# Decode hand-outs of a hybrid decoder step: 28 places for the first sequence's key pages, and a later start of the second set

## The chip, the cores and the metric

The kernel runs on one core of a Trainium2 chip. The time is device microseconds (us) of one execution. The engines of a core work from queues of their own and meet through semaphores: TensorE (PE, matrix products and transposes; PEld is its weight load), VectorE (DVE), ScalarE (ACT), GpSimd (POOL), and SyncE (SP), which here issues most DMA transfers. The profiler also shows the clock that TensorE was granted (PEclk, 1.00 is full).

## The reference

A step of a two-layer decoder: 1024 prompt tokens with 16 meta tokens in front, and 8 running sequences with one new token each. Layer 0 mixes by gated linear attention (GLA), layer 1 by differential attention; each is followed by a squared-ReLU MLP, and each sum by a LayerNorm:

```
x = post_norm(x, mixer(x), ln_mix_g, ln_mix_b)      # layer_norm(ALPHA*x + f)
x = post_norm(x, relu(x @ w1)**2 @ w2, ln_mlp_g, ln_mlp_b)
...
k_past = cache_k[page_table].reshape(B, past, DIFF_HEADS, 2, DIFF_DH)
v_past = cache_v[page_table].reshape(B, past, DIFF_HEADS, DIFF_DV)
o = diff_core(q, [k_past | k], [v_past | v], ...)   # both softmaxes, then their difference
```

The part that the change touches is the last of these for the 8 running sequences ("decode"): each has 32 pages of 128 past keys and 32 pages of values, 1024 float32 numbers to a row, in a cache that a page table addresses. That is 256 key pages and 256 value pages of 512 KB each. The scores are taken against one query row, softmax goes over all 4096 past positions and the own one, and the values are summed with the weights.

## The kernel before

**Order of the program.** First GLA and the few-token work of the running sequences (through both layers up to the projections of layer 1, so that decode's queries exist early), then for the prompt: `w_out` of GLA (L887), a LayerNorm (`normalize`), the first MLP (`mlp`, L978), a LayerNorm, layer 1's projection (the loop over 12 units of 256 columns that ends with `next(paged, None)`), the prompt's attention (`prep` and `tile_`, from L1105 on), and layer 1's own output product and MLP. Products are made in float32 out of three passes (`mm3`, L185 to L188): each operand is split into a high and a low part, the rest is taken by a subtraction (`split`, L183 on DVE: `XH`/`XL` for activations, `HH`/`HL` for the MLP's hidden values; for weights L174 on POOL, `wlo`, after ACT's L173, `whi`).

**Decode runs beside this work.** `decode()` (L848) is a generator. For each sequence b it makes `k_start` (the query row `qb` in all partitions), the softmax of the sequence before it (`soft`, L792), and then 32 turns. A turn takes one key page of b and one value page of b-1. A key page (`k_page`, L782) is a DMA of 512 KB through SP, whose address SP reads from the page table first (L756, then L758), one product with the query (L789; on POOL for every fourth page, otherwise on DVE), and one reduction to 16 scores (L790, on DVE). A value page is one DMA and four matmuls of 256 columns (`v_pages`, L830), issued for two pages at a time and tied behind the key reduction of the same turn. Key and value pages share one pool (`pgp`) of 8 tiles. After the last sequence `v_end` (L836) moves the sums out; the pool is given back (`de.close()`) before the prompt's attention begins, whose buffers lie in the same room.

**What sets the order.** A scheduler lays the instructions of each engine out by priority and by its own reckoning of when each could start. Nearly all of decode stands at a priority behind everything else ("background"), so that it fills what others leave. Two things pull it back:

- *Hand-outs.* At a `yield` the generator stops until the main program calls `next` on it. `w_out` calls it after each of its first 5 tiles, the first down run of the MLP after every second of its 16 tiles (8 calls), and then `next(x for x in side if x)` lets decode run without a stop until the next `yield` that gives a nonzero b. Between that and the next place, decode is "free": its pages are issued in one go, at background priority. The projection hands out one turn per tile from its first tile on, and what is left after the last `yield` is free again.
- *Order behind a step.* `tc.issue_after(ins)` keeps an instruction behind `ins` in the schedule. A handed-out page's product stands behind the newest entry of `steps_v` (DVE's steps of the main program) or `steps_g` (POOL's).

The hand-outs are: pages 0 to 11 of sequence 0 at 13 places (5 and 8); pages 12 to 199 free, in the first MLP; pages 200 to 215 (sequence 6, turns 8 to 23) at 16 places in the projection; pages 216 to 255 and the value pages of the last sequence free after that. `HOLD = (6, 8)` says where the second set begins.

**Other lines that matter below.** In the MLP's first round (`g == 0`) DVE also multiplies the residual `Y` by `ln_mix_g` (`alpha_row`, L970), four times two instructions, each pair after a DMA of a row of weights into `ht`, which has one buffer. The LayerNorm takes statistics of `Y` on DVE (L923, L927, L931), a power on POOL (L932), the shift on DVE (L936), and applies both on ACT (L938). PE then transposes the result (L949), which ACT or DVE (L953) scale and DVE splits (L183). L1014 adds a product to `Y` in the MLP's down runs. `prep` (L1105) transposes keys and queries of a head on PE (L1134 for the 16 meta rows, L1139 keys, L1144 queries) with a `split` behind each; `tile_` multiplies them (L1174 to L1176) into scores, which DVE masks (L1182) with the tile `cmask`, set at L1102 in room that decode had.

Of the kernel before, what the change touches and what calls it, by code (L numbers as in the profile page):

```python
# [30 lines left out]
NPG = 32  # L31
# [2 lines left out]
NEG = -1e30  # L34
LAM_INIT = 0.8 - 0.6 * math.exp(-0.3)
PGB = 8
HOLD = (6, 8)
HTB = 1
LEVELS = (64, 32, 16, 8, 4, 2, 1)
ROPE_INV = 500000.0 ** (-np.arange(0, 16, 2, dtype=np.float64) / 16)  # L40
# [70 lines left out]
def hybrid_step(ctx, tc, A, dbg=None, upto=9):  # L111
# [69 lines left out]
    def split(hi, lo, src, eng=V):  # L181
        S.copy(hi, src)
        return eng.tensor_tensor(lo, src, hi.bitcast(F32), op=ALU.subtract)  # L183
# [55 lines left out]
    ps = smt()  # L239
# [15 lines left out]
    for c in range(2):  # L255
        for k in range(NB):
            ps = axt()
            for i in range(4):
                TE.transpose(ps[:, i * P : (i + 1) * P], Yt[:, 4 * c + i, k * P : (k + 1) * P], ident)
            cs = slice(512 * c, 512 * c + 512)  # L260
# [13 lines left out]
    ps = smt()  # L274
# [46 lines left out]
    for c in range(2):  # L321
        ps = mmt()
# [55 lines left out]
    ps = smt()  # L378
# [4 lines left out]
    ps = smt()  # L383
# [8 lines left out]
    ps = smt()  # L392
# [4 lines left out]
    for h in range(GH):  # L397
        m = log_gate(ps[:, h * TS : (h + 1) * TS], TS, h)
# [23 lines left out]
    ps = smt()  # L422
# [5 lines left out]
    for hh in range(2):  # L428
        ps = smt()
# [8 lines left out]
    ps = smt()  # L438
# [4 lines left out]
    for s in (8, 4, 2, 1):  # L443
        u = t2()[:, :128]
        level(sb.rearrange("p h t -> p (h t)"), sqk[:, :128], sqk[:, 128:], u, s, V)
        ps = smt()
# [46 lines left out]
    ps = smt()  # L493
# [61 lines left out]
    for half in range(2):  # L555
        ps = smt()
# [54 lines left out]
    for h in range(GH):  # L611
# [7 lines left out]
        for c in range(2):  # L619
            q, k_, v = qk[c, 0], qk[c, 1], Yh[:, h, 4 * c : 4 * c + 4, :]  # L620
            cs = slice(512 * c, 512 * c + 512)
            m = log_gate(pgs[c], 512, h)
            b = g2.tile([P, 512], F32, name="gb")
# [159 lines left out]
    def k_page(b, n, sc, qb):  # L783
        with background():
            pg = page("cache_k", b, n)
            eng, after = (G, steps_g) if n % 4 == 3 else (V, steps_v)

            with tc.issue_after(after[-1]) if (b == 0 and n < 24 and after) or (b == HOLD[0] and HOLD[1] <= n) else nullcontext():
                eng.tensor_tensor(pg, pg, qb, op=ALU.mult)  # L789
            return V.tensor_reduce(sc[:, n, :], pg.rearrange("p (h d) -> p h d", d=64), op=ALU.add, axis=AX.X).ins  # L790

# [56 lines left out]
    def decode():  # L848
        ks = None
        for b in range(NS + 1):  # L850
            prev = ks
            if b < NS:
                ks = k_start(b)
            if b > 0:
                w = soft(prev[0])
                acc = smt()
            held, k = [], None
            for n in range(NPG):
                if b == 0 or (b == HOLD[0] and HOLD[1] <= n < HOLD[1] + 16):
                    yield b  # L860
                if b < NS:
                    k = k_page(b, n, *ks)
                if b > 0:

                    if len(held) == 2:
                        v_pages(held, w, acc, k)
                        held = []
                    held.append((n, v_load(b - 1, n)))
            if b > 0:
                held.append((NPG, v_load(b - 1, NPG)))  # L870
                v_pages(held, w, acc, None)
                v_end(b - 1, acc)
# [9 lines left out]
    def w_out(w, scaled, side=None):  # L882

        units = {}
        n = 0
        for u, c in ((0, 0), (1, 0), (0, 1), (1, 1), (2, 0), (3, 0), (2, 1), (3, 1)):
            if u not in units:  # L887
                units[u] = kunit(w, u * 256)
            hv, lv = (x.rearrange("p (k n) -> p k n", n=256) for x in units[u])
            for i2 in range(2):  # L890
                ps = mmt()
                t0 = 4 * c + 2 * i2
                for i in range(2):
                    a = slice((t0 + i) * P, (t0 + i + 1) * P)
                    for k in range(NB):
                        mm3(ps[:, i * 256 : (i + 1) * 256], XH[:, k, a], XL[:, k, a], hv[:, k, :], lv[:, k, :], k == 0, k == NB - 1)
                yv = Yt[:, t0 : t0 + 2, u * 256 : (u + 1) * 256]
                pv = ps.rearrange("p (i n) -> p i n", n=256)
                if scaled:
                    V.tensor_tensor(yv, yv, pv, op=ALU.add)  # L900
                else:
                    steps_v.append(V.scalar_tensor_tensor(yv, yv, ALPHA, pv, ALU.mult, ALU.add).ins)
                if side and (n == 4 if scaled else n < 5):
                    next(side)
                n += 1
                if u % 2:
                    for t in (t0, t0 + 1):
                        yield t, u // 2
# [66 lines left out]
    def mlp(side):  # L975

        w1, w2 = A["mlp_w1"][0], A["mlp_w2"][0]
        for g in range(8):  # L978
            us = [None, None]
            order = [(u, c) for c in range(2) for u in range(2)] if g == 0 else [(u, c) for u in range(2) for c in range(2)]  # L980
            for u, c in order:
                if us[u] is None:
                    us[u] = kunit(w1, g * 512 + u * 256)
                hv, lv = (x.rearrange("p (k n) -> p k n", n=256) for x in us[u])
                cs = slice(512 * c, 512 * c + 512)
                for m in range(2):
                    ps = mmt()
                    ms = slice(m * P, (m + 1) * P)
                    for k in range(NB):
                        mm3(ps, hv[:, k, ms], lv[:, k, ms], XH[:, k, cs], XL[:, k, cs], k == 0, k == NB - 1)  # L990
                    S.activation(ps, ps, AF.Relu)
                    S.activation(ps, ps, AF.Square)
                    split(HH[:, 2 * u + m, cs], HL[:, 2 * u + m, cs], ps)
            if g == 0:
                with tc.issue_after(steps_v[-1]):
                    list(alpha_row(A["ln_mix_g"][0:1], ALU.mult))
                beta = alpha_row(A["ln_mix_b"][0:1], ALU.add)
            elif g < 5:
                next(beta)
            us = [None, None]  # L1000
            if g < 7:
                order = [(u, t) for u in range(2) for t in range(8)]
            else:
                order = [(u, t) for u in range(2) for t in range(4)] + [(u, t) for t in range(4, 8) for u in range(2)]
            for n, (u, t) in enumerate(order):
                if us[u] is None:
                    us[u] = unit(512, w2[g * 512 : (g + 1) * 512, u * 512 : (u + 1) * 512].rearrange("(k p) n -> p k n", p=P))
                hv, lv = (x.rearrange("p (k n) -> p k n", n=512) for x in us[u])
                ps = mmt()
                ts_ = slice(t * P, (t + 1) * P)  # L1010
                for k in range(4):
                    mm3(ps, HH[:, k, ts_], HL[:, k, ts_], hv[:, k, :], lv[:, k, :], k == 0, k == 3)
                yv = Yt[:, t, u * 512 : (u + 1) * 512]
                steps_v.append(V.tensor_tensor(yv, yv, ps, op=ALU.add).ins)  # L1014
                if g == 0 and n % 2 == 0:
                    next(side, None)
                if g == 7:
                    yield t, u
            if g == 0:
                next(x for x in side if x)  # L1020
# [551 lines left out]
```

## Time and profile before

| | |
|---|---|
| time, 3 runs (us) | median 2921.13 (2912.52 to 2928.78) |
| profiled execution, its span (us) | 2919.7 |
| PE busy | 2779.7 (95%) |
| DVE busy | 1891.2 (65%) |
| ACT busy | 1044.1 (36%) |
| POOL busy | 1133.7 (39%) |
| DMA | 636.46 MB, mean 218 GB/s |
| 256 key pages, 256 value pages | 512.0 KB each, 6.0 us from issue to landing (median) |
| POOL's page products, L789 | 64, 158.6 us, mean 2478 ns |
| DVE's page products, L789 | 192, 256.8 us, mean 1343 ns |
| DVE's page reductions, L790 | 256, 309.7 us, mean 1214 ns |

The busy share of PE is an average over stages: where PE is the bound, nothing that another engine does costs time; the time that decode costs shows as idle time of PE, as a lowered clock after it, and as decode's own matmuls. By the line numbers, `w_out` and its LayerNorm run up to about 640 us, the first MLP from there to about 1457 us, the projection from about 1457 to 1785 us, and the attention begins at 1785 us. Line numbers in the profile before are those of the code above; in the changed kernel, lines from 994 on lie 4 higher (L1014 becomes L1018, L1139 becomes L1143, L1174 becomes L1178).

### The profile page before, as it was taken

How to read it: one execution, taken by the hardware profiler on the slowest of the kernel's cores; microseconds unless marked ns; L12 is line 12 of the kernel's file. 1: busy time of each engine (PE TensorE's matmuls, PEld its weight loads, DVE VectorE, ACT ScalarE, POOL GpSimd, SP SyncE). 2: the span in 40 equal slices, each digit the busy share in tenths (PEclk: the TensorE clock that was granted, in tenths of full speed). 3: DMA queues.
4: the chain of work that ended last, by engine and by line, in shares of the span. 5: the costliest groups of instructions: out<-in, count | busy, mean ns of one | idle time of the engine just before them, and what ended most of it. 6: DMA issues, size and time to landing. Idle time of an engine off the chain costs nothing. (4 is left out here: it accounts for less than half of the span.)

```text
span 2919.7 us, 52085 instructions
## 1 busy us (share of the span) xinstructions
PE 2779.7 (95%) x19653; PEld 2277.6 (78%) x19653; DVE 1891.2 (65%) x2982; ACT 1044.1 (36%) x2075; POOL 1133.7 (39%) x867
## 2 busy tenths in 40 slices
PE   8889999999999999999999998889998999999997
PEld 5666767987777777777898896778888889797885
DVE  2564644457877777777667942788638855838478
ACT  3233453251222122122321112667524535335352
POOL 2230222233333334334233331132335766677664
PEclk9899999999999999999999998999999999999998
DMA  7557651514798988988387999363436778595893
GB/s 257 178 185 251 233 177 37 198 56 141 242 350 297 335 309 298 346 317 321 137 275 252 348 343 314 75 139 86 119 112 205 195 207 232 152 281 129 257 246 87
DMA packets 285366, 636.46 MB, mean 218 GB/s; under 512 B 25510, under 2 KB 141292, under 8 KB 273852
## 3 DMA queue, kind: packets, MB, share of 16 engines
q1 hardware_dynamic: 252716, 520.66, 51.6%
q0 software_dynamic: 32400, 112.50, 15.9%
q8 instruction: 154, 2.52, 0.4%
q14 instruction: 96, 0.79, 0.1%
HBM read 575.55 MB, written 44.06 MB: 212 GB/s over the span
## 5 line engine op out<-in xcount | busy, mean ns | idle before, releaser
L174 POOL TENSOR_TENSOR wlo<-raw,whi 128x512 fp32r<-128x512 f32 x256 | 360.0, 1419 | 744.0 <-ACT whi L173 670.8
L186 PE MATMUL mmt<-whi,XH 128*128 128x256 f32 (+1 forms) x1760 | 527.4, 302 | 2.9 <-ACT Y L310 2.0
L187 PE MATMUL mmt<-wlo,XH 128*128 128x256 f32 (+1 forms) x1760 | 527.8, 301 | 0.7 <-POOL wlo L174 0.7
L186 PE MATMUL mmt<-XH,whi 128*128 128x512 f32 (+1 forms) x1216 | 438.1, 361 | 7.4 <-DVE HL L183 7.2
L188 PE MATMUL mmt<-whi,XL 128*128 128x256 f32 x1536 | 437.2, 286 | 0.1
L188 PE MATMUL mmt<-XH,wlo 128*128 128x512 f32 (+1 forms) x1216 | 434.4, 358 | 0.0
L790 DVE TENSOR_REDUCE sc<-pg 128x16 f32<-128x1024 f32 x256 | 309.7, 1214 | 93.4 <-POOL pg L789 90.1
L173 ACT CAST whi<-raw 128x512 fp32r<-128x512 f32 x256 | 152.9, 619 | 578.4 <-PE mmt L188 191.1
L186 PEld LDWEIGHTS mmt<-whi,XH 128*128 128x128 f32 x1760 | 333.4, 190 | 30.1 <-issue 15.6
L187 PEld LDWEIGHTS mmt<-wlo,XH 128*128 128x128 f32 x1760 | 334.8, 190 | 28.2 <-issue 16.8
L187 PE MATMUL mmt<-XL,whi 128*128 128x512 f32 x768 | 307.3, 400 | 0.0
L188 PEld LDWEIGHTS mmt<-whi,XL 128*128 128x128 f32 x1536 | 292.1, 191 | 9.9 <-issue 8.8
L789 DVE TENSOR_TENSOR pg<-pg,qb 128x1024 f32<-128x1024 f32 x192 | 256.8, 1343 | 62.1 <-DMA pg<-in_cache_k 38.1
L186 PEld LDWEIGHTS mmt<-XH,whi 128*128 128x128 f32 x1216 | 231.7, 191 | 55.1 <-issue 13.7
L789 POOL TENSOR_TENSOR pg<-pg,qb 128x1024 f32<-128x1024 f32 x64 | 158.6, 2478 | 293.5 <-DMA pg<-in_cache_k 236.7
L188 PEld LDWEIGHTS mmt<-XH,wlo 128*128 128x128 f32 x1216 | 231.8, 191 | 35.8 <-issue 3.8
L186 PE MATMUL mmt<-whi,HH 128*128 128x512 f32 x512 | 205.6, 402 | 1.7 <-DVE Y L1014 1.7
L187 PE MATMUL mmt<-wlo,HH 128*128 128x512 f32 x512 | 204.7, 400 | 0.0
L188 PE MATMUL mmt<-whi,HL 128*128 128x512 f32 x512 | 203.9, 398 | 0.0
L187 PEld LDWEIGHTS mmt<-XL,whi 128*128 128x128 f32 x768 | 145.4, 189 | 39.6 <-issue 8.8
L1416 POOL TENSOR_TENSOR wlo<-RW,whi 128x512 fp32r<-128x512 f32 x96 | 156.3, 1749 | 37.1 <-ACT whi L1415 37.0
L1416 POOL TENSOR_TENSOR wlo<-rw,whi 128x512 fp32r<-128x512 f32 x92 | 147.7, 1674 | 41.4 <-ACT whi L1415 41.2
(441 smaller groups left out, 5769.3 us busy)
## 6 DMA issues: line engine op xcount, KB each, us to landing
pg<-in_cache_k SPq DMA_DIRECT2D x256, 512.0 KB, 6.0
pg<-in_cache_v SPq DMA_DIRECT2D x256, 512.0 KB, 6.0
XH<-xc POOLq DMA_DIRECT2D x42, 1032.0 KB, 7.9
raw<-in_mlp_w SPq DMA_DIRECT2D x164, 256.0 KB, 3.5
swt<-in_mlp_w SPq DMA_DIRECT2D x32, 1024.0 KB, 5.6
rw<-in_mlp_w SPq DMA_DIRECT2D x116, 256.0 KB, 3.8
RW<-in_mlp_w POOLq DMA_DIRECT2D x96, 256.0 KB, 6.0
xc<-XH POOLq DMA_DIRECT2D x14, 1032.0 KB, 6.8
```

The source lines that it names most:

```text
L173: S.copy(hi[:, c], raw)
L174: G.tensor_tensor(lo[:, c], raw, hi[:, c].bitcast(F32), op=ALU.subtract)
L186: TE.matmul(ps, ah, bh, start=first, stop=False)
L187: TE.matmul(ps, ah, bl, start=False, stop=False)
L188: TE.matmul(ps, al, bh, start=False, stop=last)
L789: eng.tensor_tensor(pg, pg, qb, op=ALU.mult)
L790: return V.tensor_reduce(sc[:, n, :], pg.rearrange("p (h d) -> p h d", d=64), op=ALU.add, axis=AX.X).ins
L1416: G.tensor_tensor(lo[:, k, :], t, hi[:, k, :].bitcast(F32), op=ALU.subtract)
```

## The change

```diff
-HOLD = (6, 8)
+HOLD = range(232, 248)
...
-            with tc.issue_after(after[-1]) if (b == 0 and n < 24 and after) or (b == HOLD[0] and HOLD[1] <= n) else nullcontext():
+            with tc.issue_after(after[-1]) if (b == 0 and n < 28 and after) or HOLD.start <= NPG * b + n < NPG * (HOLD.start // NPG + 1) else nullcontext():
                 eng.tensor_tensor(pg, pg, qb, op=ALU.mult)
...
-                if b == 0 or (b == HOLD[0] and HOLD[1] <= n < HOLD[1] + 16):
+                if b == 0 or NPG * b + n in HOLD:
                     yield b
...
-                if side and (n == 4 if scaled else n < 5):
+                if side and (n == 4 if scaled else n < 12):
                     next(side)
...
         for g in range(8):
             us = [None, None]
+            normed = steps_v[-1]
...
                     S.activation(ps, ps, AF.Square)
-                    split(HH[:, 2 * u + m, cs], HL[:, 2 * u + m, cs], ps)
+                    i = split(HH[:, 2 * u + m, cs], HL[:, 2 * u + m, cs], ps).ins
+                    if g == 0:
+                        steps_v.append(i)
+                        next(side)
             if g == 0:
-                with tc.issue_after(steps_v[-1]):
+                with tc.issue_after(normed):
                     list(alpha_row(A["ln_mix_g"][0:1], ALU.mult))
```

`w_out` hands out after its first 12 tiles, the MLP's first up run after each of its 8 tiles, its first down run after 8 tiles as it did. So 28 places, after which pages 0 to 26 are issued and the free run goes from page 27 to page 231. The second set, 16 places at the same tiles of the projection, is pages 232 to 247 (sequence 7, turns 8 to 23), and 248 to 255 with the last sequence's values come free after it. The up run's subtractions become steps behind which a page's product may stand, and `normed` keeps the L970 rows behind the step that they stood behind before, the last before the MLP. The amount of work is the same.

What stands in the queues, at three places (buffer numbers in the names are the program's).

PE at the end of the projection, before: the last L186 to L188 rows are the projection's, `smt<-pg,sc` at L830 are value pages (four matmuls each), L1134 to L1144 head 0's and then head 1's transposes.

```order
L188 MATMUL mmt<-whi,XL_86 128x256
L1134 MATMUL axt<-c_ident,whi 128x16
L1139 MATMUL axt<-c_ident,wlo 128x128 x4
L830 MATMUL smt<-pg,sc 16x256 x4
L1144 MATMUL axt<-c_ident,wlo 128x128 x4
L830 MATMUL smt<-pg,sc 16x256 x4
L1139 MATMUL axt<-c_ident,wlo 128x128 x4
L830 MATMUL smt<-pg,sc 16x256 x4
L1144 MATMUL axt<-c_ident,wlo 128x128 x4
L830 MATMUL smt<-pg,sc 16x256 x4
L1174 MATMUL mmt<-XH_83 128x352
```

And in the changed kernel:

```order
L188 MATMUL mmt<-whi,XL_86 128x256
L1138 MATMUL axt<-c_ident,whi 128x16
L1143 MATMUL axt<-c_ident,wlo 128x128 x4
L1148 MATMUL axt<-c_ident,wlo 128x128 x4
L1143 MATMUL axt<-c_ident,wlo 128x128 x4
L1148 MATMUL axt<-c_ident,wlo 128x128 x4
L1178 MATMUL mmt<-XH_83 128x352
```

No value page is left behind the projection; the last ones stand before its last 912 matmuls.

DVE in the MLP's first up run, before (HL at L183 is what PE's down run waits for, L970 the residual's rows):

```order
L183 TENSOR_TENSOR HL<-mmt,HH 128x512
L953 TENSOR_SCALAR axt<-axt,lnp 128x512
L183 TENSOR_TENSOR XL_86<-axt,XH_84 128x512 x2
L970 SCALAR_TENSOR_TENSOR Y<-Y,ht 128x4x256 x6
L183 TENSOR_TENSOR HL<-mmt,HH 128x512 x2
L970 SCALAR_TENSOR_TENSOR Y<-Y,ht 128x4x256 x2
L183 TENSOR_TENSOR HL<-mmt,HH 128x512
L1014 TENSOR_TENSOR Y<-Y,mmt 128x512
```

And in the changed kernel:

```order
L789 TENSOR_TENSOR pg<-pg,qb 128x1024
L953 TENSOR_SCALAR axt<-axt,lnp 128x512
L790 TENSOR_REDUCE sc<-pg 128x16
L183 TENSOR_TENSOR XL_86<-axt,XH_84 128x512
L790 TENSOR_REDUCE sc<-pg 128x16
L183 TENSOR_TENSOR XL_86<-axt,XH_84 128x512
L970 SCALAR_TENSOR_TENSOR Y<-Y,ht 128x4x256 x2
L790 TENSOR_REDUCE sc<-pg 128x16
L970 SCALAR_TENSOR_TENSOR Y<-Y,ht 128x4x256 x4
L183 TENSOR_TENSOR HL<-mmt,HH 128x512 x2
```

Page products and reductions now stand among the splits of the up run, ahead of the L970 rows and of two HL.

DVE at the end of the first MLP, before, the rows from the last L1014 to the last L936 (the LayerNorm of the last two row blocks):

```order
L1014 TENSOR_TENSOR Y<-Y,mmt 128x512
L923 BN_STATS bst<-Y 128x6
L953 TENSOR_SCALAR axt<-axt,lnp 128x512
L927 BN_AGGR bmv<-bst 128x2
L183 TENSOR_TENSOR XL_85<-axt,XH_83 128x512
L931 TENSOR_SCALAR brs<-bmv 128x2
L183 TENSOR_TENSOR XL_85<-axt,XH_83 128x512
L936 SCALAR_TENSOR_TENSOR brs<-bmv,brs 128x2
```

And in the changed kernel, the last 12 of the 19 rows of the same stretch:

```order
L183 TENSOR_TENSOR XL_85<-axt,XH_83 128x512
L802 TENSOR_TENSOR sc<-sc,smt 128x528
L923 BN_STATS bst<-Y 128x6
L183 TENSOR_TENSOR XL_85<-axt,XH_83 128x512 x2
L790 TENSOR_REDUCE sc<-pg 128x16
L789 TENSOR_TENSOR pg<-pg,qb 128x1024
L927 BN_AGGR bmv<-bst 128x2
L804 TENSOR_REDUCE mx<-sc 128x16
L790 TENSOR_REDUCE sc<-pg 128x16
L931 TENSOR_SCALAR brs<-bmv 128x2
L789 TENSOR_TENSOR pg<-pg,qb 128x1024
L936 SCALAR_TENSOR_TENSOR brs<-bmv,brs 128x2
```

Pages and a softmax (L802, L804) of decode now stand between the steps of this LayerNorm; before, decode's free run had ended at page 199 ahead of it.

## The prediction, made before the changed kernel ran

> **What bounds the kernel now.** The page's busy shares come first: PE is busy 95% of the span, so only the rest, and PE time at a lowered clock, can be won. Next the windows of 50 us, to find the stages in which PE rests:
>
> ```profile
> core 0: us, PE busy (x) PEld busy (x) DVE busy (x) ACT busy (x) POOL busy (x), PEclk, DMA share, GB/s
> 700.00:750.00 50.00, 45.84 (x191) 36.46 (x190) 47.12 (x39) 14.88 (x26) 26.54 (x12) 0.97 0.56 189
> 1400.00:1450.00 50.00, 50.00 (x274) 39.84 (x273) 31.79 (x58) 15.95 (x22) 10.57 (x9) 1.00 0.31 112
> 1550.00:1600.00 50.00, 47.44 (x415) 40.83 (x414) 46.73 (x60) 9.04 (x18) 16.93 (x12) 0.93 0.78 263
> 1600.00:1650.00 50.00, 47.25 (x410) 43.84 (x410) 39.23 (x56) 7.85 (x14) 14.09 (x8) 0.93 0.94 328
> 1750.00:1800.00 50.00, 44.63 (x441) 33.37 (x440) 6.33 (x11) 7.76 (x15) 1.28 (x1) 0.98 1.00 352
> ```
>
> PE is full in 1400 to 1450, while DVE has 18 us to spare and the DMA share is 0.31: decode's free run has ended there, and nothing of it is done until the projection. From 1550 on DVE and DMA are loaded again, PE loses 2.6 and 2.8 us to idleness in two windows, and at the end, 1750 to 1800, the DMA share is 1.00 at 352 GB/s: the last values come in as fast as they ever do. So decode sets the end of this stage. Who is waited for stands in the waits of PE, of 700 to 800, 1550 to 1600, 1600 to 1650 and 1800 to 1830:
>
> ```profile
> PE mmt L186 <- DVE HL L183: 5.2, 3, 3.8
> PE mmt L186 <- DVE Y L1014: 1.7, 2, 1.3
> ...
> PE smt L830 <- DMA pg<-in_cache_v: 2.6, 1, 2.6
> ...
> PE smt L806 <- DVE mx L804: 2.7, 1, 2.7
> ...
> PE axt L1139 <- DVE XL L183: 7.3, 1, 7.3
> ```
>
> Each has decode behind it. The clock falls with them (windows around each, and the end of the stage):
>
> ```profile
> 724.00:733.00 9.00, 5.91 (x20) 4.76 (x21) 9.00 (x10) 1.13 (x2) 2.38 (x1) 0.81 0.92 335
> 1584.00:1594.00 10.00, 7.43 (x53) 4.73 (x51) 9.74 (x9) 2.76 (x5) 6.75 (x6) 0.66 0.90 331
> 1612.00:1621.00 9.00, 6.25 (x30) 6.15 (x30) 9.00 (x14) 1.62 (x3) 5.21 (x3) 0.62 0.73 240
> 1785.00:1815.00 30.00, 18.24 (x176) 9.55 (x174) 6.76 (x16) 6.87 (x15) 5.31 (x11) 0.78 1.08 319
> 1815.00:1826.00 11.00, 11.00 (x47) 9.24 (x48) 8.56 (x33) 6.80 (x15) 1.02 (x2) 0.52 0.86 159
> ```
>
> **The tail behind the projection.** PE's timeline there, and two neighbouring matmuls of the projection:
>
> ```profile
> 1785.06 0.23 PE L1134 MATMUL axt<-c_ident,whi 16*128 16x16 f32 x1
> 1789.98 0.42 PE L1174 MATMUL mmt<-XH 64*128 64x352 f32 x1
> 1791.61 1.92 PE L830 MATMUL smt<-pg,sc 128*16 128x256 f32 x32
> 1802.62 1.12 PE L1139 MATMUL axt<-c_ident,wlo 128*128 128x128 f32 x4 [7.35 <-DVE XL L183]
> 1810.14 1.18 PE L830 MATMUL smt<-pg,sc 128*16 128x256 f32 x16 [0.85 <-DMA pg<-in_cache_v]
> 1814.89 0.66 PE L1174 MATMUL mmt<-XH 64*128 64x352 f32 x1 [1.17 <-DVE ast L1182]
> ...
> 1456.55 0.28 PE L187 MATMUL mmt<-wlo,XH 128*128 128x256 f32 x1
> 1456.67 0.28 PE L188 MATMUL mmt<-whi,XL 128*128 128x256 f32 x1
> ```
>
> Head 0's first nine products ran by 1791.6, but their masking, and all that follows, came at 1814.9. The wait for XL is decode too: DVE stood at `cmask`, which lies in decode's room and could be set only when SP had read the addresses of the last pages (the first row is DVE's, the second PE's value matmuls alone):
>
> ```profile
> 1802.22 0.33 DVE L1102 MEMSET cmask<- 128x320 f32 x1 [11.56 <-SPq L756]
> ...
> 1785.00:1815.00 30.00, 10.37 (x128) 3.37 (x128) 0.78 1.08 319
> ```
>
> In the changed queue no L830 stands behind the projection, and the last stands 912 matmuls ahead of its end, some 109 us at the 0.12 us at which the projection's matmuls follow each other. So even if the last values come tens of us late, `cmask` finds its room free. What it is worth: of the 30 us, PE rested 30 - 18.24 = 11.8. Head 0 still needs its own transposes and splits before a product, and the 2.5 us of value matmuls that filled its gaps are gone, so about 2.3 us of rest stays: 9.5 saved. The 10.37 us of value matmuls are not saved; they move into the projection, where PE is the bound. The lowered clock behind the rests goes with them: (1 - 0.78) x 18.24 = 4.0 here, of which I take 3.5, and (1 - 0.52) x 11 = 5.3 in the window after, of which I take half, 2.6, since that stretch waits for DVE as well. **Tail: -15.6**, between -9.5 (rests alone) and -19 (all of it).
>
> **The two rests in the projection.** 2.6 + 2.7 us idle, and by the clock (1 - 0.66) x 10 + (1 - 0.62) x 9 = 6.8, of which 0.7 fell in the rest itself: 11.4 in all. The first is a value page that came late, the other the softmax of sequence 6 behind page reductions on DVE. After the change only 24 key pages are left for the projection instead of 56, so DVE is nearly free there and the second has no ground. But the values of the last two sequences still come one page after another, and 42 of them are used within 624 of the projection's matmuls, 75 us plus their own PE time; at 512 KB that is 21.5 MB in about 100 us, 215 GB/s beside the projection's weights: under the 352 shown, not far under with the weights on top. I let one of the two stay: **-5.7**, between -11.4 and +3 (both stay, and a third of the same kind comes).
>
> By the page TensorE: Matmul & The Clock Gate of the Trainium skill (Part 1, the HAM clock gate) the clock goes to half after an idle window of about 3.4 us; here rests of 2.6 and 2.7 us had it at 0.66 and 0.62, so the trace is harsher. By that rule the two would be worth their 5.3 us of rest alone, and the term about -2.7.
>
> **The early stage.** The free run of sequence 0 in the first down run vanishes from that place. DVE there, before:
>
> ```profile
> 707.23 13.57 DVE L789 TENSOR_TENSOR pg<-pg,qb 128x1024 f32<-128x1024 f32 x8
> 720.73 5.71 DVE L790 TENSOR_REDUCE sc<-pg 128x16 f32<-128x1024 f32 x5
> ```
>
> 19 us of pages stood ahead of an HL, and PE waited 3.8 us for it. All the rests in 700 to 800 are 5.2 + 1.7 = 6.9, and the clock of 724 to 733 adds (1 - 0.81) x 9 = 1.7: **-8.6** if they all go, which needs the next burst, at page 27, to meet PE with more in hand. Against it stands the up run, which hands out eight pages now. Its DVE already makes PE wait:
>
> ```profile
> 655.74 0.50 PE L186 MATMUL mmt<-XH,whi 128*128 128x512 f32 x1 [2.01 <-DVE HL L183]
> ...
> 641.46 2.35 DVE L970 SCALAR_TENSOR_TENSOR Y<-Y,ht 128x1024 f32<-128x1024 f32 x2
> 647.06 2.36 DVE L970 SCALAR_TENSOR_TENSOR Y<-Y,ht 128x1024 f32<-128x1024 f32 x2 [3.24 <-DMA ht<-in_ln_mix_g]
> 652.72 2.36 DVE L970 SCALAR_TENSOR_TENSOR Y<-Y,ht 128x1024 f32<-128x1024 f32 x2 [3.31 <-DMA ht<-in_ln_mix_g]
> ```
>
> The L970 pairs come 5.6 us apart, each after a row of weights that could be fetched only when the pair before had left the one buffer `ht`, and DVE's queue is strict: an HL behind the third pair waits for it, and PE behind that. What the change puts ahead of them costs:
>
> ```profile
> L789 DVE TENSOR_TENSOR pg<-pg,qb x192: 1155/1218/2940, 539.5 to 1733.5; 128x1024 f32<-128x1024 f32 x192
> L790 DVE TENSOR_REDUCE sc<-pg x256: 1170/1219/1223, 540.7 to 1740.2; 128x16 f32<-128x1024 f32 x128
> ```
>
> Before the first L970 pair the queue now has several of these between splits; some run where DVE rested, and I put the pairs 5.3 us later, about four of them. The HL behind the third pair comes at 661 instead of 655, and PE waits about 7.5 us, 5.5 more than before, with 2 us of clock after it and 1 us for the pages between the first L1014: +8.5. It is bounded by 0 (pages wholly in DVE's rests) and +16 (eight pages' six products and eight reductions on DVE, 17.1 us, all but 1 us of it in the way). **Early stage: 0**, from -8 to +8. If the cover fails, that is, if PE has no matmul that needs no HL, this term is the one that grows.
>
> **The end of the first MLP.** Here the free run now reaches page 231, and decode fills what was empty:
>
> ```profile
> 1400.00:1457.00 57.00, 34.49 (x62) 1.00 0.32 111
> ...
> 1447.89 0.69 DVE L1014 TENSOR_TENSOR Y<-Y,mmt 128x512 f32<-128x512 f32 x1 [0.92 <-PE mmt L188]
> 1453.05 1.25 DVE L936 SCALAR_TENSOR_TENSOR brs<-bmv,brs 128x2 f32<-128x2 f32 x1 [0.85 <-POOL brs L932]
> ...
> 1454.33 2.38 ACT L938 ACTIVATE Y<-Y,brs 128x1024 f32<-128x1024 f32 x2 [2.33 <-DVE brs L936]
> ...
> 1456.79 0.49 PE L949 MATMUL axt<-c_ident,Y 128*128 128x128 f32 x3
> ```
>
> Before, 5.2 us lay between the last L1014 and the last L936 on DVE, then 2.4 us of ACT, and PE found the rows ready. In the changed queue the same stretch has five L790 (6.1), three L789 (3.7) and two softmax steps more (about 1.0 together, from the smaller rows): 16 us instead of 5.2, 10.8 later. The changed order puts PE's L949 behind 38 more matmuls of the projection, 4.5 us. So PE waits 6.3, and with the clock after it **+7**; between +1 (the pages come while DVE rests anyway, 22.5 us of the 57) and +12 (nothing is covered). Late next is the split of these transposes, so the projection's second half, which comes 48 matmuls to a tile and has room.
>
> On these two terms a rule speaks against the change: the page SBUF — State Buffer of the Trainium skill (SBUF: two separate sides) says that a DVE operation with two inputs in SBUF and a GpSimd operation that reads SBUF exclude each other on a shared port pair. The trace agrees as far as the eight L789 at 707 go, 1.70 us each instead of 1.22, in a stage with POOL's `wlo`. By the rule three L789 at 2.9 us would make the last term +12 and no more.
>
> **Sum.** -15.6 - 5.7 + 0 + 7 = -14.3 against the profiled execution's 2919.7: 2905.4. The median of the runs is 1.4 above that execution, so about **2906**.
>
> **Rivals.**
> - *Everything goes and nothing comes.* DVE's rests take the pages of both MLP ends: -15.6 - 11.4 - 8.6 + 5 (for what of them cannot) = -31, about **2889**. For it speaks the spare DVE time of 1400 to 1457; against it that DVE's order is fixed and its LayerNorm rows stand behind pages.
> - *The tail's gain is eaten.* The tail at its low end, -9.5, the two rests stay, +1 early, +7 at the LayerNorm: -1.5, about **2919**. For it speaks the DMA share of 0.9 to 1.0 from 1600 on.
> - *Slower: the LayerNorm at the end of the first MLP is starved by pages on DVE.* The free run did 188 pages in some 700 us, 15 in 57 us; at 2.4 us each that is 37 us, and 34.5 of 57 are taken, so 14 us do not fit. If they all fall into the chain of the last LayerNorms, with L789 at 1.70 (+7) and the extra 10.8 in the last stretch, and the clock after (+7), it costs 39; with the tail's -15.6, the early term at +8, the rests' -11.4: +20, **2940**. It decides from 41.6 us of new waits on, counted against tail and rests (27.0 + 14.6).
> - *It does not do what it says*: the last values still come behind the projection, for DMA was the bound there; then about **2921**. Against it stands the new order of PE, 109 us of slack.
>
> **How the numbers follow.** A measurement here can tell about 0.5% (14.6 us) from no change: faster is under 2906.5, slower over 2935.7. The forecast has 0.42; its own range is 2896 to 2917, so it lies astride that bound, 0.23 faster and 0.19 the same. Everything goes: 0.27, faster. Eaten, or not done: 0.14, the same. The starved LayerNorm: 0.17, slower. So faster 0.50, the same 0.33, slower 0.17. The range goes from 2884 (the first rival without its 5) to 2932 (between the forecast's top and the starved LayerNorm), and leaves out the worse part of the starved LayerNorm and a little of the first rival.
>
> **What the changed profile would show.** Right: at the end of the projection no L830, and from the last L188 to the masked products of L1182 (now 4 lines on) some 7 us instead of 30, at a clock near 1.00; in 1400 to 1457 DVE well over 34.5 us busy; at some 655 to 662 a wait of PE for HL of 5 to 9 us; in 700 to 750 PE above 45.8 us. Wrong: a wait of PE behind DVE at L949 or L183 of over 15 us near 1457; a wait for `pg<-in_cache_v` of over 5 us in the projection; `cmask` still released by SP late.

## The result, and the profile after

| | before | changed |
|---|---|---|
| median of 20 runs each (us) | 2921.69 (2912.46 to 2929.30) | 2925.90 (2920.95 to 2936.86) |
| ratio to before | | 1.0017, 95% interval 1.0007 to 1.0028 |
| profiled execution, its span (us) | 2919.7 | 2920.6 |
| DVE busy (us) | 1891.2 | 1872.0 |
| POOL busy (us) | 1133.7 | 1140.9 |

Nothing was won, and 4 to 5 us were lost. The windows of the changed kernel, in the order of the columns that the prediction shows, with one more at the end for the 30 us after the projection:

```profile
700.00:750.00 50.00, 49.84 (x252) 38.65 (x251) 40.13 (x40) 13.68 (x24) 18.77 (x11) 1.00 0.56 182
1400.00:1450.00 50.00, 50.00 (x296) 35.77 (x294) 45.85 (x56) 10.42 (x14) 14.66 (x10) 1.00 0.89 319
1450.00:1500.00 50.00, 40.63 (x288) 30.98 (x285) 43.12 (x71) 22.56 (x37) 20.76 (x15) 0.86 0.76 258
1500.00:1550.00 50.00, 47.98 (x429) 44.54 (x429) 33.08 (x55) 11.49 (x20) 12.61 (x8) 1.00 0.91 316
1550.00:1600.00 50.00, 50.00 (x449) 46.98 (x449) 31.79 (x46) 8.45 (x15) 15.15 (x10) 1.00 0.78 245
1600.00:1650.00 50.00, 47.13 (x421) 41.20 (x424) 38.20 (x57) 9.22 (x18) 14.44 (x10) 0.97 0.83 294
1750.00:1800.00 50.00, 50.00 (x426) 50.00 (x425) 0.00 (x0) 7.47 (x13) 5.31 (x5) 1.00 0.35 108
1809.30:1839.30 30.00, 26.51 (x119) 22.37 (x119) 18.58 (x56) 13.97 (x31) 4.86 (x9) 0.60 0.94 212
```

The early stage is full (49.84 of 50 instead of 45.84), the end of the projection is full with DVE at rest (decode is done), and behind the projection PE rests 3.5 us of 30 instead of 11.8. The loss is one new hole: 1450 to 1500, where PE does 40.6 of 50 at a clock of 0.86. PE's waits from 1457 to 1516 (us in total, times, longest):

```profile
PE axt L949 <- DVE XL L183: 3.4, 2, 2.9
PE axt L949 <- ACT Y L938: 2.7, 2, 2.1
PE mmt L188 <- DVE XL L183: 2.0, 2, 1.3
PE mmt L186 <- DVE Y L1018: 0.9, 1, 0.9
PE mmt L187 <- POOL wlo L174: 0.8, 2, 0.6
PE smt L801 <- DVE m L799: 0.8, 1, 0.8
PE mmt L186 <- ACT whi L173: 0.4, 1, 0.4
PE mmt L186 <- ACT XH L182: 0.2, 1, 0.2
```

Twelve rests, 11.2 us in all, 9.2 of them on the MLP's sums, the LayerNorm and the splits behind it. DVE in that place, its windows and then four rows of its timeline:

```profile
1400.00:1457.00 57.00, 52.85 (x65) 1.00 0.87 308
1457.00:1515.00 58.00, 46.65 (x75) 0.88 0.82 284
...
1473.33 0.67 DVE L1018 TENSOR_TENSOR Y<-Y,mmt 128x512 f32<-128x512 f32 x1
1478.69 1.20 DVE L789 TENSOR_TENSOR pg<-pg,qb 128x1024 f32<-128x1024 f32 x1
...
1488.83 1.85 DVE L789 TENSOR_TENSOR pg<-pg,qb 128x1024 f32<-128x1024 f32 x1 [1.39 <-DMA pg<-in_cache_k]
1491.26 0.16 DVE L936 SCALAR_TENSOR_TENSOR brs<-bmv,brs 128x2 f32<-128x2 f32 x1 [0.59 <-POOL brs L932]
```

DVE is more than nine tenths full before the stretch (52.85 of 57; 34.49 before the change). From the last sum (L1018) to the last L936 pass 17.9 us instead of 5.2, and one page's product even waits there for its load, with the LayerNorm queued behind it.

Where the time went, by position in the program: the start of the main matmul (L186 to L188) that has the given number among all 12,480, in both traces, the value matmuls done by then, and PE's rest so far. Two numbers in a cell are before and changed.

| main matmul, and what lies before it | before | changed | difference | value matmuls | PE at rest |
|---|---|---|---|---|---|
| 2304: up to the first MLP | 611.1 | 612.4 | +1.3 | 0, 0 | 43.9, 44.8 |
| 5184: the first MLP without its end | 1397.2 | 1408.1 | +10.9 | 1320, 1448 | 52.8, 54.4 |
| 5568: end of the MLP, LayerNorm, first products | 1477.3 | 1516.2 | +38.9 | 1384, 1648 | 53.1, 65.8 |
| 7488: the projection but its last tiles | 1751.4 | 1786.5 | +35.1 | 1848, 2112 | 58.4, 68.7 |
| 7680: the tail, and all of the attention | 2068.2 | 2071.7 | +3.6 | 2112, 2112 | 96.5, 95.2 |

Before the change, the 616 value matmuls between 1457 and 1785 us kept PE busy for 42.0 us, so of a difference those done earlier are taken off at 0.07 us each, an estimate. The MLP's end then lost 28.0 - 9.5 = 18.5 (11.1 of rest, and 13.6 us at half clock, 6.8); the tail won 31.5 - 18.5 = 13.0; the projection won 3.8; the MLP before its end lost 9.6 - 9.0 = 0.6. Behind the table's last row the changed kernel's trace won 2.7 us back, for its whole span is only 0.9 longer. Such shares are good to some 2 us: two profiles of one and the same kernel (28 at 216, below) lie 3.4 us apart at the first row, and up to 1.7 in the stretches between the rows. Each kernel has one trace, of one execution, and that can be far from its median: with 28 at 200 and with the late pairs at 216 (both below) it took 2923.5 us, where the median is 2916.2, and with 12 places and 16 (below) 2920.1, where it is 2913.5.

### The profile page after: what moved, and what is told of

Read it like the earlier page. It is cut to its first block, busy times and chain, and to the rows that moved or that the text cites. A ratio compares the mean times of both kernels' runs of the same rounds, so it can differ in the third digit from the quotient of the medians.

```text
span 2920.6 us, 52071 instructions
## 1 busy us (share of the span) xinstructions
PE 2782.6 (95%) x19653; PEld 2271.7 (78%) x19653; DVE 1872.0 (64%) x2982; ACT 1043.8 (36%) x2075; POOL 1140.9 (39%) x867
## 5 line engine op out<-in xcount | busy, mean ns | idle before, releaser
L186 PE MATMUL mmt<-whi,XH 128*128 128x256 f32 (+1 forms) x1760 | 528.2, 301 | 6.1 <-ACT Y L310 3.0
L186 PE MATMUL mmt<-XH,whi 128*128 128x512 f32 (+1 forms) x1216 | 436.4, 360 | 6.7 <-DVE HL L183 6.3
L188 PE MATMUL mmt<-whi,XL 128*128 128x256 f32 x1536 | 437.0, 286 | 2.0 <-DVE XL L183 2.0
L188 PE MATMUL mmt<-XH,wlo 128*128 128x512 f32 (+1 forms) x1216 | 433.8, 357 | 0.0
L186 PEld LDWEIGHTS mmt<-whi,XH 128*128 128x128 f32 x1760 | 333.0, 190 | 34.0 <-issue 15.5
L789 DVE TENSOR_TENSOR pg<-pg,qb 128x1024 f32<-128x1024 f32 x192 | 263.4, 1375 | 71.6 <-DMA pg<-in_cache_k 50.8
L188 PEld LDWEIGHTS mmt<-whi,XL 128*128 128x128 f32 x1536 | 290.7, 190 | 12.9 <-issue 9.7
L186 PEld LDWEIGHTS mmt<-XH,whi 128*128 128x128 f32 x1216 | 230.3, 190 | 55.0 <-issue 15.8
L188 PEld LDWEIGHTS mmt<-XH,wlo 128*128 128x128 f32 x1216 | 230.6, 190 | 38.1 <-issue 6.4
L186 PE MATMUL mmt<-whi,HH 128*128 128x512 f32 x512 | 205.3, 401 | 3.1 <-DVE Y L1018 2.1
L188 PE MATMUL mmt<-whi,HL 128*128 128x512 f32 x512 | 204.3, 399 | 0.0
L1420 POOL TENSOR_TENSOR wlo<-RW,whi 128x512 fp32r<-128x512 f32 x96 | 157.1, 1766 | 43.9 <-ACT whi L1419 43.8
```

Source lines behind the costliest of these rows:

```text
L186: TE.matmul(ps, ah, bh, start=first, stop=False)
L188: TE.matmul(ps, al, bh, start=False, stop=last)
L1420: G.tensor_tensor(lo[:, k, :], t, hi[:, k, :].bitcast(F32), op=ALU.subtract)
```

## The experiments

All ratios are to the kernel before, with their 95% intervals. "28 at 216" stands for 28 places for sequence 0 and a second set that begins at page 216; so the kernel before is 13 at 200, the changed one 28 at 232. The start sets one thing more, by the condition in `k_page`: from it to the end of its sequence, a page's product is tied behind a step of the main program. These are 24 pages with the starts 200 and 232, 8 with 216, 16 with 208, 32 with 224.

### The grid of places and starts

```diff
-HOLD = range(232, 248)
+HOLD = range(200, 216)
```

> The changed kernel with its second set of hand-outs back at pages 200 to 215 (28 places for sequence 0 stay). Theory A (the change lost its gain in the LayerNorm at the end of the first MLP, where decode's pages stand on DVE): the queue has no page there, so the 11 us of idle PE and about 7 us of lowered clock of 1457 to 1515 are gone; the tail behind the projection is that of the kernel before, with its 11.8 us of rest. Net against before: the early part alone, -4 to +5 us, ratio 0.9985 to 1.0017. Theory B (the loss lies in the early part, in the up run that hands out eight pages): +5 us or more, ratio over 1.0017.

Measured 0.9978 (0.9963 to 0.9992). PE's rest between matmuls 5184 and 5568 was 0.2 us, so the loss at the MLP's end went as theory A had it, and by the ratio B fell. The time is a little under its range. Where that came from the trace does not show: at the projection's end it is 5 us later than before, at the first product of `w_out` 3 us earlier, and its whole span is 2 us longer than that of before.

```diff
-HOLD = range(232, 248)
+HOLD = range(216, 232)
```

> The changed kernel with the second set at pages 216 to 231. No page stands in the last LayerNorm of the first MLP, and the last value page stands 446 matmuls ahead of the projection's end. Theory A: the loss of 18 us at the MLP's end goes, the tail's gain of about 10 us and the 7 us at the two rests of the projection stay: -13 us against before, -18 against the changed kernel, ratio 0.994 to 0.9975. Rival (the tail gains nothing, since head 0's preparation bounds it and the clock stays low there anyway): -2 to +3 us, ratio 0.999 to 1.001.

Measured 0.9941 (0.9921 to 0.9962): theory A. Waits of PE from 1450 to 1510, and the window:

```profile
PE mmt L188 <- DVE XL L183: 0.3, 1, 0.3
PE mmt L187 <- POOL wlo L174: 0.2, 1, 0.2
...
1450.00:1510.00 60.00, 59.57 (x482) 54.68 (x481) 40.58 (x72) 26.38 (x42) 21.05 (x16) 1.00 0.58 187
```

Against the changed kernel the MLP's end cost nothing, and the end of the projection came at 1791.2 instead of 1809.4. The last value matmul ended at 1738.0, 53 us ahead of it, so a start 16 pages earlier still keeps the tail free. Against 28 at 232 only the one number was changed, and with it the number of tied pages; these do not make the hole, for 28 at 200 ties as many as 28 at 232 and has none.

28 at 232 with the places of before:

```diff
-            with tc.issue_after(after[-1]) if (b == 0 and n < 28 and after) or HOLD.start <= NPG * b + n < NPG * (HOLD.start // NPG + 1) else nullcontext():
+            with tc.issue_after(after[-1]) if (b == 0 and n < 24 and after) or HOLD.start <= NPG * b + n < NPG * (HOLD.start // NPG + 1) else nullcontext():
...
-                if side and (n == 4 if scaled else n < 12):
+                if side and (n == 4 if scaled else n < 5):
...
-                    i = split(HH[:, 2 * u + m, cs], HL[:, 2 * u + m, cs], ps).ins
-                    if g == 0:
-                        steps_v.append(i)
-                        next(side)
+                    split(HH[:, 2 * u + m, cs], HL[:, 2 * u + m, cs], ps)
```

> The changed kernel with 13 hand-outs as before (5 in w_out, none in the up run), second set at 232. Pages stand in the last LayerNorm of the first MLP (five reductions, four products), but no softmax does. Theory A by pages: the loss at the MLP's end is as in the changed kernel, 14 to 20 us, and the time is 0 to +6 us of before, ratio 1.000 to 1.002. Rival (the softmax of sequence 6 in that place is what costs): the loss is 5 us or less, and the time 8 us or more under before, ratio under 0.997.

Measured 1.0013 (0.9999 to 1.0027). The same window and its waits:

```profile
1450.00:1510.00 60.00, 50.29 (x399) 39.20 (x399) 52.89 (x75) 26.17 (x43) 23.64 (x16) 0.89 0.92 325
...
PE mmt L186 <- ACT XH L182: 4.9, 2, 3.1
PE axt L949 <- DVE brs L936: 1.3, 1, 1.3
PE axt L949 <- ACT Y L938: 1.3, 2, 0.8
PE axt L949 <- DVE XL L183: 1.2, 2, 0.9
PE mmt L186 <- DVE Y L1015: 1.0, 1, 1.0
```

The hole is nearly as large without the softmax: 9.7 us of rest, 13.6 us at half clock. Pages are enough.

And these 13 places with the start at 216:

```diff
-HOLD = range(232, 248)
+HOLD = range(216, 232)
```

> 13 hand-outs as before, second set at 216. One product and three reductions stand in the last LayerNorm of the first MLP. Theory A: a loss of 4 to 8 us there, the tail's -10 and the rests' -7 as with 28 places: -8 to -12 us, ratio 0.996 to 0.9975. If 28 places are needed for the tail to be free (rival), 0 us, ratio 0.999 to 1.001.

Measured 0.9983 (0.9970 to 0.9997), short of the range, but not by the rival: the last value matmul ended 53 us ahead of the projection's end. Four rows of pages in the last LayerNorm cost more than the 4 to 8 us that I gave them:

```profile
1450.00:1510.00 60.00, 52.50 (x417) 46.35 (x419) 46.05 (x73) 25.63 (x42) 20.66 (x14) 0.91 0.71 245
```

7.5 us of rest and 10.2 us at half clock: 12.6 us. So the 28 places do count: sequence 0's pages are done earlier, and fewer are left for the MLP's end.

### The work itself taken away

In the changed kernel, in `k_page`; the scores of these pages are left out:

```diff
+                if 200 <= NPG * b + n < 232:
+                    return V.tensor_copy(sc[:, n, :], pg[:, :16]).ins
                 eng.tensor_tensor(pg, pg, qb, op=ALU.mult)
```

> The changed kernel (28 places, second set at 232) in which the key pages 200 to 231 are loaded as before, but their product and reduction are left out: a copy of 16 numbers stands in their place, so the loads, the values' matmuls and the softmax of sequence 6 come as they did. Theory A (DVE's page work holds up the LayerNorm at the end of the first MLP): PE rests under 4 us in 1457 to 1515 instead of 11, the clock stays at 1.00 there, and the time is 14 to 20 us under the changed kernel, ratio to before 0.993 to 0.997. Rival (the loads, the values' matmuls or the softmax do it): 8 us or more of the 11 stay, ratio 0.999 to 1.002.

Measured 0.9977 (0.9964 to 0.9989); the trace came to matmul 5568 at 1498.2 instead of 1516.2, 14.7 us of it between 5184 and 5568, and PE's rest there fell by 9.6 us:

```profile
1450.00:1510.00 60.00, 58.18 (x497) 50.17 (x497) 42.33 (x82) 26.07 (x43) 16.19 (x12) 0.97 0.92 328
```

The loads (DMA share 0.92), the softmax and the value matmuls are all there. So the pages' work on DVE and POOL makes the hole; how much of it is POOL's was not tried apart. By the two ratios the whole is 0.4% better than the changed kernel, about 12 us, a little less than the 14 to 20 expected, and the clock was 0.97 instead of the expected 1.00.

### The clock in the tail

28 at 216, and before and in `tile_` (`last` is the ninth product of head 0's first tile):

```diff
+    def fill(n, after):
+        ps = smt()
+        with tc.issue_after(after):
+            for _ in range(n):
+                TE.matmul(ps[:, :P], ident, ident, start=True, stop=True)
...
+            if h == 0 and t == 7 and m == 0:
+                fill(12, last)
```

> 28 places, second set at 216, and 12 products of the identity with itself on PE behind head 0's first nine products, whose result is not used. The clock stood at half for 20.5 us from 1797 us on, after 3 us in which PE was busy for 1.69. Theory C (thin work of PE in that short stretch sets it off, whatever decode does): with the rest filled, the granted clock of the 20 us behind is 0.85 or more, and the time 2 to 6 us under the run without the filler. Rival (the products of head 0, which use 64 of the 128 rows, do not hold the clock up by themselves): it falls all the same, mean under 0.65 over the 20 us, and the time is the same or up to 1 us longer.

Measured 0.9932 (0.9911 to 0.9952). The window 1797 to 1817, without the filler and then with it:

```profile
1797.00:1817.00 20.00, 18.41 (x73) 15.14 (x74) 14.64 (x48) 10.63 (x24) 4.35 (x8) 0.50 0.99 222
...
1797.00:1817.00 20.00, 18.69 (x105) 14.82 (x104) 15.55 (x50) 12.56 (x30) 4.87 (x9) 0.83 0.84 178
```

The clock was 0.83 instead of 0.50, which speaks for C (0.83 is just short of its 0.85). But the last run with this filler (12 places with 16, below) speaks against it: there the clock was at half for 20.5 us again, 3.4 from 1800.3 on and 17.1 from 1814.0 on. The second fall came after a stretch in which PE was busy for 2.99 of 3.40 us:

```profile
1810.60:1814.00 3.40, 2.99 (x14) 2.09 (x14) 3.33 (x15) 2.59 (x8) 2.48 (x5) 1.00 0.93 255
1814.00:1831.10 17.10, 16.73 (x66) 13.76 (x66) 7.60 (x23) 6.80 (x17) 1.53 (x3) 0.50 0.81 148
```

So rests of PE in that place are not all that sets it off; the rival, that products with 64 of the 128 rows do not hold the clock up, stays open. In the run here, the time from the projection's end to head 2's preparation fell only from 51.0 to 48.9 us, and the ratios can't be told apart: 13.7 us less at half clock came with 2 us of time. The stretch waits for DVE, DMA and ACT as well.

### Three more ways to place the early work, and two more starts

28 at 216, and in the first round of `mlp` ("the late pairs" below):

```diff
-                with tc.issue_after(normed):
-                    list(alpha_row(A["ln_mix_g"][0:1], ALU.mult))
+                gain = alpha_row(A["ln_mix_g"][0:1], ALU.mult)
+                split_ = steps_v[-1]
+                with tc.issue_after(normed):
+                    next(gain)
+                    next(gain)
+                with tc.issue_after(split_):
+                    list(gain)
```

> 28 places, second set at 216, and the third and fourth pair of L970 (the columns that the first half of the down run does not need) put behind the last split of the first up run instead of behind the last step before the MLP. Theory A (the 6.5 us that PE waits for HL at 662 us, and the half clock after it, come from the third pair, which waits for its row of weights): the wait falls under 1.5 us, -6 to -9 us against the run with 28 places at 216, ratio to before 0.990 to 0.993. Rival (DVE is full there with pages, the wait only moves to a sum of the down run): 0 to -2 us, ratio 0.9935 to 0.996.

Measured 0.9975 (0.9964 to 0.9987): the gain did not come. Waits of PE from 640 to 800, 28 at 216 first, then this one:

```profile
PE mmt L186 <- DVE HL L183: 6.5, 1, 6.5
...
PE mmt L186 <- DVE Y L1023: 6.4, 5, 2.7
PE mmt L186 <- DVE HL L183: 2.6, 1, 2.6
```

The wait was the third pair's, for it fell to 2.6; but 6.4 us came back at the sums of the down run. The rival holds, and the time is worse still.

The same kernel with `HOLD = range(208, 224)`:

> As the run with the late pairs of L970, but the second set at pages 208 to 223. The last value page stands behind the projection again. Theory A: the tail loses 4 to 10 us, the LayerNorm at the MLP's end stays free of pages: ratio 0.993 to 0.997. Rival (nothing is late in the tail as long as most values are done): as the run at 216, within 2 us.

Measured 0.9981 (0.9971 to 0.9991). The last value matmul ended at 1795.1, behind the projection's end at 1793.2. The run that differs in the start alone is the late pairs at 216, and by the ratios (0.9981 and 0.9975) the two can't be told apart, which fits the rival. In the traces, the time from the projection's end to head 2's preparation is 54.1 us against 49.9, theory A's 4 us, but the rest of the attention is 9 us shorter, so the price of the late values is not settled. And with `HOLD = range(224, 240)`:

> As the run with the late pairs of L970, but the second set at pages 224 to 239. In the last stretch of the first MLP's LayerNorm stand two steps of a softmax and no page; among the last eight sums of the down run six reductions and four products. Theory A by pages ahead of the LayerNorm: 4 to 9 us of new waits at the MLP's end, ratio 0.993 to 0.996. Rival (only pages between the last sum and the last L936 cost): within 2 us of the run at 216.

Measured 0.9988 (0.9973 to 1.0003). Between matmuls 5184 and 5568 PE rested 4.4 us against 0.9 with the late pairs at 216: theory A in the trace. By the ratios these two can't be told apart either. Both times are above their ranges, which were set from an expected gain that the run before did not show.

28 at 216 without the up run's places:

```diff
-                    i = split(HH[:, 2 * u + m, cs], HL[:, 2 * u + m, cs], ps).ins
-                    if g == 0:
-                        steps_v.append(i)
-                        next(side)
+                    split(HH[:, 2 * u + m, cs], HL[:, 2 * u + m, cs], ps)
```

> Second set at 216, 12 places in w_out, none in the first up run, 8 in the first down run: 20 in all. Theory A: PE's wait for HL in the up run is 2 us again instead of 6.5, but sequence 0's burst in the down run costs 4 to 7 us again, and five products and eight reductions stand among the last eight sums of the MLP (1 to 5 us): 0 to +7 us against 28 places, ratio 0.994 to 0.998. Rival (the up run's wait is all that counts): -5 to -9, ratio 0.991 to 0.9935.

Measured 0.9996 (0.9983 to 1.0009), above the range. Up to the projection's end it is level with 28 at 216 (1789.2 against 1791.2 and, in a second profile, 1789.3): PE's wait for HL was 2.0, the burst cost 3.2, and the MLP's end some 5 us more. The rest came in the attention (271.4 us against 259.1 and 260.8).

The same with the 12 products of `fill`, and in the first down run:

```diff
-                if g == 0 and n % 2 == 0:
+                if g == 0:
```

> Second set at 216, 12 places in w_out, none in the up run, 16 in the first down run (one after each tile), and the 12 products without use behind head 0's. If the up run's wait can be had back without the burst: 4 to 7 us under the run with filler and 28 places, ratio 0.9905 to 0.9925. Rival (one page to a tile is more than DVE has room for in the down run, so that PE waits for the sums there): no gain, ratio 0.9925 to 0.997.

Measured 0.9973 (0.9957 to 0.9988): just above the rival's range, and no gain. The wait for HL was 2.2 us, a sum of the down run was waited for 2.4, and the projection ended at 1795.8.

Last, 28 at 216 once more, on another chip:

> 28 places, second set at 216, once more, on the chip of the three runs beside it: ratio 0.992 to 0.996 if the first measurement holds; over 0.997 if it was the luck of six runs.

Measured 0.9961 (0.9948 to 0.9974): a smaller gain than the 0.9941 of the first six runs, but not over the 0.997 that would have made it luck. 28 at 216 beats the kernel before by 0.4 to 0.6% and the changed one by 0.6 to 0.8%.

### What is left open

The attention of three kernels (the late pairs, 20 at 216, and 12 places with 16) lasted 270 to 271 us from the projection's end to the first product of `w_out`, that of 28 at 216 259.1 and 260.8. The scheduler lays the attention out anew for each program: its instructions stand in another order, on POOL and SP too, whose queues move the heads' operands. Where the order is the same on all engines, or all but the same, it lasted 259.1, 260.8 and 262.3 (28 at 216 twice, 13 at 216), and in another order 266.5 and 270.2 (13 at 232, the late pairs): up to 4 us apart within an order, 4 to 11 between these two. With the late pairs and the start at 224 it was 257.3, so the late pairs as such do not make it long. PE's waits for such moves, in the attention of 28 at 216 and then of the late pairs:

```profile
PE mmt L1182 <- DMA XH<-XH: 2.7, 1, 2.7
...
PE mmt L1187 <- DMA XH<-XH: 3.1, 1, 3.1
...
PE mmt L1188 <- DMA XL<-XL: 2.1, 1, 2.1
```

That explains a part of the 11 us only. Two of the three long attentions, those of the late pairs and of 12 places with 16, stand in traces that lie some 7 us above their kernel's median. I made no run that changes the order of the attention alone, so how much of a ratio comes from there is not settled: some 4 us of the change's own tail may be of this kind too, since from head 2's preparation on it took 209.6 us instead of 213.9. With 28 at 216 it took 208.1 and 209.2, so some 5 us of that version's gain may be of this kind.

## Why the prediction was wrong

The forecast was 2906, faster by 14 us; it came out 4 to 5 us slower. That this lies inside the range is owed to the range's width. The nearest case was "the tail's gain is eaten" with its 2919, though it was not eaten by what that case named; what ate it is the mechanism of the starved LayerNorm, at half the 39 us of that case.

**The end of the first MLP: +7 forecast, +18.5 measured.** This is the step that failed, beyond its upper bound of +12. The length of the last stretch was well forecast (16 us, 17.9 measured). The wait priced from it, L949 for ACT's L938, was even shorter than forecast: 2.7 instead of 6.3. What was missed stands in the other rows of the waits: 8.5 us more, mostly for splits and sums around it, each a little late, with DVE's queue more than nine tenths full from 1400 on. The sign that the prediction set for this, one wait of over 15 us, did not come: the longest was 2.9. And I gave the clock less than 1 us, where 13.6 us at half speed cost 6.8. I had the number that says so, 15 pages at 2.4 us each into 22 us of spare DVE, and used it for a rival only, not for the term. That the pages' work does it is shown by three runs: 28 at 216 (no page there, no hole), 13 at 232 (no softmax there, nearly the same hole), and the loads without their products (15 of the 18 us gone).

**The tail: -15.6 forecast, about -13 measured, inside its bounds.** No value page stood behind the projection, `cmask` still waited for SP, but long before it was needed, and the masked products came 6.8 us after the projection instead of 29:

```profile
1677.74 0.33 DVE L1106 MEMSET cmask<- 128x320 f32 x1 [3.05 <-SPq L756]
...
1812.86 0.43 PE L1178 MATMUL mmt<-XH 64*128 64x352 f32 x1 [0.68 <-ACT XH L182]
1816.08 0.26 PE L1138 MATMUL axt<-c_ident,whi 16*128 16x16 f32 x1 [1.54 <-DMA whi<-out_k_rows_p]
...
1816.19 0.52 DVE L1186 CUSTOM_DVE_ANT_0 as<-mmt,cmask 128x352 f32<-128x352 f32 x1 [2.66 <-DMA whi<-out_k_rows_p]
```

The rests gave 11.6 by the table (the attention's among them) instead of 9.5. The clock gave nothing of its 6.1: it stood at half for 23.9 us before and for 23.9 us after. So it falls in the heads' preparation without decode's rests too, and in the run with filler 13.7 us less of it came with only 2 us of time.

**The rests in the projection: -5.7 forecast, -3.8 measured.** As forecast one of the two stayed, a value page's, 2.5 us. By the rest (2.9 us in the stretch instead of 5.3) and the clock (3.4 us at half instead of 13.6) 7.5 should have been won; where the other 3.7 went is not shown. The Trainium skill's rule of an idle window of about 3.4 us (TensorE: Matmul & The Clock Gate, Part 1, the HAM clock gate) would have let the clock stand. The trace has it at half for 3.4 us after this rest, and before the change for 6.8 after each of the two.

**The early stage: 0 forecast, about +1 measured.** Both halves were there. PE waited for an HL behind the third pair of L970, 6.27 us in place of 2.01:

```profile
661.13 0.80 PE L186 MATMUL mmt<-XH,whi 128*128 128x512 f32 x1 [6.27 <-DVE HL L183]
```

and of the 6.9 us of rest in 700 to 800 0.9 was left.

## What to carry to other kernels

A stretch of a queue that is more than nine tenths full (52.85 of 57 us here) is not priced by the longest interval in it: much in it comes a little late, and the clock behind many small waits costs again, so count what does not fit. Where background work is moved into an empty place, ask whether the place was empty because nothing in it can wait; here the same pages some tens of us later cost next to nothing. And a change to the program of one stage may lay out the next one anew, so look whether the stages that should be equal are.

## What the runs showed of the hardware that was not expected

TensorE's clock fell to half after a stretch in which PE was never at rest for longer than 1.4 us: in 28 at 216 from 1797 on, after 3 us with PE busy for 1.69, and it stayed there for 20.5 us though PE was busy for 18.9 of them, in good part with products that use 64 of the 128 rows:

```profile
1794.00:1797.00 3.00, 1.69 (x10) 1.40 (x9) 1.18 (x2) 0.59 (x1) 0.00 (x0) 1.00 1.16 321
1797.00:1817.50 20.50, 18.91 (x75) 15.64 (x76) 15.02 (x50) 10.68 (x24) 4.35 (x8) 0.50 1.01 223
```

With 2.5 us of products of full size in the gap it was at half for 6.8 us only, but with the same products in another run for 20.5, and 17.1 of them began at 1814.0 after 3.4 us in which PE was busy for 2.99 and never at rest for longer than 0.2. So short rests alone do not explain it; whether it is the size of the products was not tried apart.
